# Attention scores of a hybrid decoder block: two 128-row matmuls per head become three pairs of 64-row matmuls, one head in each half of the array

## The chip, the cores and the metric

The kernel runs on one core of one Trainium2 chip (trn2). The metric is the device time of one execution in microseconds (us). Five engines work side by side: TensorE (PE) for matrix products, with its weight loads shown apart as PEld, VectorE (DVE), ScalarE (ACT), GpSimd (POOL) and SyncE (SP), which here only issues DMAs.

## The reference, cut to what matters

One decoder block on 2048 positions and 1024 channels. Two branches are computed from one input projection, gated, merged, projected and normalised. The part that is changed is the score product of the attention branch:

```python
q, k, v, g_attn, u_lru, g_lru, gate_logits = jnp.split(x @ w_in[l] + b_in[l], SPLIT_POINTS, axis=-1)
q, k = rope(q), rope(k)                     # 3 groups x 8 heads x 64 channels
for g, (window, dilation) in enumerate(((128, 1), (512, 4), (2048, 16))):
    # positions regrouped by residue mod dilation, blocks of 128 queries
    # against [previous block, current block] of keys
    s = jnp.einsum('brnqhd,brnkhd->brnhqk', qb, kw) * (Dh ** -0.5)
    s = jnp.where(valid, s, NEG_INF)
    m = jnp.max(s, -1); p = jnp.exp(s - m); l = jnp.sum(p, -1)
    o = jnp.einsum('brnhqk,brnkhd->brnqhd', p, vw) / l
# groups combined by their softmax weights, times silu(g_attn), projected;
# branch B: conv, gated linear recurrence; merge, output projection, layer norm
```

## The kernel before

The kernel has three stages. In the first (`product`, L583), PE multiplies x by the input projection, tile by tile of 128 x 512, each float32 operand split into a high and a low part of type fp32r, so that a product is three matmuls (high x high, high x low, low x high). The loop over `where` (L904 on) goes in ticks of 12 matmuls; a planner with budgets per engine (`left`, `Ask`, `chains`) places what follows each tile: rotary rotation, splits, stores to scratch in DRAM. q is stored there already split (`qh`, `ql`), k whole (`k`).

The second stage is the attention. A *unit* u is one pair of heads of one group, 12 units in the order of groups 0, 2, 1 (`unit`, L764). Each has 16 query blocks, so there are 192 steps, with m = 16u + n. In the loop at L1061 step m issues, in program order,

- `step_s(m)`: the scores of block n for both heads into PSUM, then on DVE the mask and row minimum (L977), on ACT the exponential (L979);
- `step_t(m-3)`: transposes of the 128 x 128 blocks of p on PE (L988) and their copy out of PSUM, by ACT (L993) or DVE (L995);
- `step_v(m-4)`: the products with v in float32, two instructions each (L1012), a copy every second step (L1016) and a store to `o_scr` every fourth (L1026).

A block with a previous block has 256 keys and twice the transposes and products with v. A block without one, and every block of group 2, has 128; in group 2 the score matmul still writes 256 columns.

For the scores, each head has its own full-height operands. `A[:, h]` holds `qh` of head h in its 64 partitions and `ql` in the other 64. `B1[:, h]` holds the high part of k in both halves, and `b2[:, h]` the low part of k in the head's half and zeros in the other. So two matmuls over 128 rows give qh·kh + ql·kh and qh·kl (L973). The zeros are written once (L780, L781). The k of a unit is loaded half by half into `b2`; POOL makes the high part (L792), copies it across (L793) and subtracts (L795), each on 64 x 1024 elements; for the first head of unit 0 ACT and DVE do that (L788, L789, L795).

Slots of SBUF are named by hand (`USLOT`, L757): three per unit, two units held. The parts of unit u+1 are queued in `loads` at n = 0 of unit u and one is issued per step (L1070 to L1075), since their slots are those of unit u-1. The first loads are issued in the last seven ticks of the first stage (L917), where slots become free as the x blocks in them are used for the last time, and just ahead of the loop (L1057): unit 1's q, then the v of group 2. All of these go through SP's queue in program order. `later(n, fn)` runs fn n ticks or steps on; the splits of k run 3 and 4 after their load. PSUM has three buffers for scores (both heads in one bank), three for transposes and two for o.

The third stage (`yb_job`, `combine`, `ya_job`, `out_job`) takes the slots X0 to X5 again; its first weights and inputs are loaded during unit 11 (L1076 to L1081).

Of the kernel before, what the change touches and what calls it, by code (L numbers as in the profile page):

```python
# [15 lines left out]
P = 128  # L16
# [15 lines left out]
def hybrid_block_kernel(ctx: ExitStack, tc: tile.TileContext, a: dict, out: bass.AP):  # L32
# [3 lines left out]
    def flat(t):  # L36
        return t.bitcast(F32)
# [45 lines left out]
    def big(slot, shape, dt, name):  # L83
        return (Y if slot[0] == "Y" else Z if slot[0] == "Z" else X).tile(shape, dt, name=name, tag=slot)
# [671 lines left out]
    lo_, up_ = slice(0, 64), slice(64, P)  # L756
    USLOT = (("X4", "X3", "X2"), ("Y0", "X1", "X0"))  # L757
    VSLOT = {(0, 0): "X5", (2, 0): "Y1", (1, 0): "Y2", (0, 1): "X5", (2, 1): "Y1", (1, 1): "Y2"}
    zero = [False, False]
    B2 = {}  # L760
# [7 lines left out]
    def unit_parts(u):  # L768

        sl = USLOT[u % 2]  # L770
        g, hp = unit(u)
        q = {n: qk_scr[n, 4 * g + hp] for n in ("qh", "ql", "k")}

        def k_part(h, hs, os):
            def fn():
                if h == 0:
                    units[u] = [None, big(sl[1], [P, 2, S], F32R, f"B{u}")]
                    if u < 2:
                        B2[u] = big(sl[2], [P, 2, S], F32R, f"C{u}")
                        pool.memset(flat(B2[u][up_, 0]), 0.0)  # L780
                        pool.memset(flat(B2[u][lo_, 1]), 0.0)  # L781
                    units[u].append(B2[u % 2])
                _, B1, b2 = units[u]
                sp.dma_start(flat(b2[hs, h]), q["k"][hs])

                def split(t):
                    if (u, h) == (0, 0):
                        act.activation(B1[hs, h, t], flat(b2[hs, h, t]), AF.Copy)  # L788
                        act.activation(B1[os, h, t], flat(B1[hs, h, t]), AF.Copy)  # L789
                        eng = dve  # L790
                    else:
                        pool.tensor_copy(B1[hs, h, t], flat(b2[hs, h, t]))  # L792
                        pool.tensor_copy(B1[os, h, t], flat(B1[hs, h, t]))  # L793
                        eng = pool
                    eng.tensor_tensor(out=b2[hs, h, t], in0=flat(b2[hs, h, t]), in1=flat(B1[hs, h, t]), op=ALU.subtract)  # L795

                later(3, lambda: split(slice(0, S // 2)))
                later(4, lambda: split(slice(S // 2, S)))
            return fn

        def q_part(hs, h, n, qs):
            def fn():
                if (hs, h) == (lo_, 0):
                    units[u][0] = big(sl[0], [P, 2, S], F32R, f"A{u}")
                sp.dma_start(flat(units[u][0][hs, h]), q[n][qs])
# [96 lines left out]
    first, second, firstv = unit_parts(0), unit_parts(1), v_parts(0, 0)  # L902
# [48 lines left out]
    def step_s(m):  # L951
        u, n = divmod(m, 16)
        g, _ = unit(u)
        A, B1, b2 = units[u]
# [6 lines left out]
        for h in range(2):  # L961
            q = A[:, h, n * P:(n + 1) * P]
            for i, B in enumerate((B1, b2)):
                if g == 2:
                    k = B[:, h].rearrange("p (c r i) -> p r c i", c=4, r=16)[:, max(n - 1, 0):n + 1]
                elif pv is None:
                    k = B[:, h, n * P:(n + 1) * P]
                elif g == 0:
                    k = B[:, h, (n - 1) * P:(n + 1) * P]
                else:  # L970
                    c, r = divmod(n, 4)
                    k = B[:, h, (c - 1) * CH:(c + 1) * CH].rearrange("p (c r j) -> p r c j", c=2, r=4)[:, r]
                pe.matmul(s[:, h, (0 if g == 2 and n else lo):256], q, k, start=(i == 0), stop=(i == 1))  # L973
        p = at_p.tile([P, 2, 256], F32, tag="p", name=f"p{m}", bufs=5)
        for h in range(2):
            mm = osb[:, n % 4, 130 + h:131 + h]
            dve.tensor_tensor_reduce(out=p[:, h, lo:256], in0=s[:, h, lo:256], in1=mask[:, lo:256],  # L977
# [79 lines left out]
    for fn in second[2:] + v_parts(2, 0):  # L1057
        fn()
    VORD = {0: (1, 0), 4: (0, 1), 5: (2, 1), 6: (1, 1)}
    loads = []  # L1060
    for m in range(NB + 4):  # L1061
# [8 lines left out]
        if n == 0 and 1 <= u <= 10:  # L1070
            loads += unit_parts(u + 1)
# [360 lines left out]
```

## Time and profile before

| | us |
|---|---|
| median of 3 runs | 2267.64 (2267.12 to 2272.91) |
| span of the profiled execution | 2268.7 |
| PE busy | 2213.9 (98%) |
| DVE busy | 1752.4 (77%) |
| ACT busy | 1091.3 (48%) |
| POOL busy | 874.6 (39%) |
| first to last score matmul | 1480.4 to 1807.6 |

The profiled execution is one run under the profiler. Its span, from the first to the last instruction, is the time that is known of it; it stands 1.1 us above the median of the runs. A matmul's duration runs from its start to a modelled end and overlaps the next one's, so the distance between starts, and not the duration, tells what a matmul costs in a dense row.

### The profile page before, as it was taken

How to read it: one execution, taken by the hardware profiler on the slowest of the kernel's cores; microseconds unless marked ns; L12 is line 12 of the kernel's file. 1: busy time of each engine (PE TensorE's matmuls, PEld its weight loads, DVE VectorE, ACT ScalarE, POOL GpSimd, SP SyncE). 2: the span in 40 equal slices, each digit the busy share in tenths (PEclk: the TensorE clock that was granted, in tenths of full speed). 3: DMA queues.
4: the chain of work that ended last, by engine and by line, in shares of the span. 5: the costliest groups of instructions: out<-in, count | busy, mean ns of one | idle time of the engine just before them, and what ended most of it. 6: DMA issues, size and time to landing. Idle time of an engine off the chain costs nothing.

```text
span 2268.7 us, 34220 instructions
## 1 busy us (share of the span) xinstructions
PE 2213.9 (98%) x11032; PEld 1868.7 (82%) x11032; DVE 1752.4 (77%) x3234; ACT 1091.3 (48%) x1982; POOL 874.6 (39%) x640
## 2 busy tenths in 40 slices
PE   7999999999999999999999999989999999999998
PEld 6888878888787788888888888878999888788887
DVE  8788878999898877778778878655666668967777
ACT  5344545456455656556566566555666621121010
POOL 1545544555454022222222212257676426722220
PEclk9999999999999999999999999999999999999999
DMA  7998897988987777686888787897786679884441
GB/s 227 268 259 254 244 266 222 273 267 269 273 266 249 258 215 225 201 241 208 252 276 258 249 250 237 251 256 176 206 217 160 191 234 316 287 271 167 130 140 65
DMA packets 327954, 526.01 MB, mean 232 GB/s; under 512 B 97120, under 2 KB 138080, under 8 KB 322912
## 3 DMA queue, kind: packets, MB, share of 16 engines
q1 hardware_dynamic: 297008, 479.05, 68.1%
q0 software_dynamic: 10080, 18.35, 5.1%
q10 hardware_dynamic: 20688, 26.42, 3.7%
q8 instruction: 88, 1.44, 0.3%
q14 instruction: 90, 0.74, 0.1%
HBM read 318.38 MB, written 190.64 MB: 224 GB/s over the span
## 4 chain that ended last, share of the span: by engine, by line
PE 57%; DMA 6%; DVE 2%; ACT 1%; POOL 1%; issue 1%; SPq 1%; ACTq 0%; DVEq 0%; POOLq 0%
PE q L598 29%; PE o L1012 4%; PE s L973 3%; PE z L1304 2%; PE z L1305 2%; PE z L1303 2%; PE yb L1198 2%; PE yb L1200 2%; PE yb L1199 2%; PE pt L988 2%; DMA A<-qh_scr 2%; PE ya L1271 1%; PE ya L1272 1%; PE ya L1270 1%; DMA l<-wl_scr 1%
## 5 line engine op out<-in xcount | busy, mean ns | idle before, releaser
L598 PE MATMUL q<-xT,hS 128*128 128x512 f32 x1680 | 520.9, 391 | 7.2 <-ACT e L621 6.0
L598 PE MATMUL q<-xT,l 128*128 128x512 f32 x1120 | 437.1, 390 | 0.0
L598 PE MATMUL q<-xB,hA 128*128 128x512 f32 x1248 | 389.7, 394 | 10.1 <-ACT xB L202 5.7
L598 PEld LDWEIGHTS q<-xT,hS 128*128 128x128 f32 x1680 | 314.9, 188 | 73.0 <-ACT e L621 6.4
L598 PE MATMUL q<-xB,l 128*128 128x512 f32 x904 | 354.6, 392 | 1.4 <-DMA l<-wl_scr 1.3
L598 PEld LDWEIGHTS q<-xB,hA 128*128 128x128 f32 x1248 | 234.7, 189 | 61.0 <-ACT xB L202 5.7
L598 PEld LDWEIGHTS q<-xT,l 128*128 128x128 f32 x1120 | 210.7, 188 | 44.1
L979 ACT ACTIVATE p<-p,osb 128x256 f32<-128x256 f32 (+1 forms) x384 | 156.2, 454 | 118.4 <-DVE osb L977 117.7
L214 POOL TENSOR_TENSOR S<-S,wA 128x512 f32<-128x512 f32 x35 | 45.7, 1306 | 422.6 <-DVE S L214 251.7
L977 DVE CUSTOM_DVE_ANT_0 p<-s,mask 128x256 f32<-128x256 f32 (+1 forms) x384 | 125.2, 364 | 103.0 <-PE s L973 61.5
L598 PEld LDWEIGHTS q<-xB,l 128*128 128x128 f32 x904 | 171.0, 189 | 38.5 <-DMA l<-wl_scr 2.2
L214 POOL TENSOR_TENSOR sw<-sw,sin 128x512 f32<-128x512 f32 x96 | 161.8, 1691 | 70.3 <-DMA sw<-y 64.6
L259 ACT ACTIVATE hA<-wA 128x512 fp32r<-128x512 f32 x218 | 135.5, 624 | 89.6 <-DMA wA<-in_w_in_dram 52.7
L598 PE MATMUL q<-xB,hS 128*128 128x512 f32 x560 | 174.9, 394 | 3.0 <-DVE v L214 3.0
L598 PE MATMUL q<-xT,hA 128*128 128x512 f32 x560 | 173.1, 390 | 3.1 <-ACT hi L323 1.8
L1012 PE MATMUL o<-V,ptb 128*128 128x65 f32 x1200 | 166.4, 277 | 8.0 <-ACT ptb L993 5.3
L1012 PEld LDWEIGHTS o<-V,ptb 128*128 128x128 f32 x1200 | 153.3, 196 | 19.4 <-ACT ptb L993 16.2
L259 ACT ACTIVATE hS<-S 128x512 fp32r<-128x512 f32 x175 | 109.2, 624 | 97.1 <-DVE S L214 51.3
L214 POOL TENSOR_TENSOR l<-wA,hA 128x512 fp32r<-128x512 f32 x68 | 105.2, 1547 | 80.3 <-ACT hA L259 61.6
L973 PE MATMUL s<-B,A 128*128 128x256 f32 (+1 forms) x384 | 116.8, 326 | 10.0 <-DMA A<-qh_scr 6.4
L598 PEld LDWEIGHTS q<-xT,hA 128*128 128x128 f32 x560 | 104.6, 188 | 26.6 <-issue 3.7
L598 PEld LDWEIGHTS q<-xB,hS 128*128 128x128 f32 x560 | 104.7, 189 | 25.1 <-issue 4.1
(196 smaller groups left out, 4853.0 us busy)
## 6 DMA issues: line engine op xcount, KB each, us to landing
wA<-in_w_in_dram SPq DMA_DIRECT2D x253, 256.0 KB, 5.0
wl_scr<-l SPq DMA_DIRECT2D x105, 512.0 KB, 5.3
l<-wl_scr SPq DMA_DIRECT2D x105, 512.0 KB, 4.7
sw<-y SPq DMA_DIRECT2D x384, 64.0 KB, 3.3
wS<-in_w_in_dram SPq DMA_DIRECT2D x70, 256.0 KB, 4.7
wS<-in_w_in_dram POOLq DMA_DIRECT2D x70, 256.0 KB, 6.6
o_scr<-osb ACTq DMA_DIRECT2D x48, 264.0 KB, 5.9
oc<-o_scr SPq DMA_DIRECT2D x48, 264.0 KB, 5.0
```

The lines of the kernel that those rows point to most:

```text
L214: eng.tensor_tensor(out=out, in0=in0, in1=in1, op=op)
L259: act.activation(h, r, AF.Copy)
L598: pe.matmul(bank, w[:, ks], x[:, kk, xx], start=(first and i == 0), stop=(last and i == 11))
L973: pe.matmul(s[:, h, (0 if g == 2 and n else lo):256], q, k, start=(i == 0), stop=(i == 1))
L977: dve.tensor_tensor_reduce(out=p[:, h, lo:256], in0=s[:, h, lo:256], in1=mask[:, lo:256], scale=1.0, scalar=3e38, op0=ALU.add, op1=ALU.min ...
L979: act.activation(p[:, h, lo:256], p[:, h, lo:256], AF.Exp, scale=-1.0, bias=mm)
L988: pe.transpose(pt[:, 2 * h + x, :], p[:, h, x * P:(x + 1) * P], ident)
L1012: pe.matmul(o[:, n % 2, h * 65:h * 65 + 65], ptb[:, 2 * h + x, :], V[:, kb, vo + h * 65:vo + h * 65 + 65], start=(x == lo // P), stop=(x = ...
L1198: pe.matmul(yb, WL[f][:, 0, k], xx[:, 0], start=(k == 0), stop=False)
L1199: pe.matmul(yb, WL[f][:, 0, k], xx[:, 1], start=False, stop=False)
L1200: pe.matmul(yb, WL[f][:, 1, k], xx[:, 0], start=False, stop=(k == 7))
L1303: pe.matmul(z, mh[:, k], w[:, 0, hs], start=(k == 0), stop=False)
```

## The change

The operands of a unit become two tiles of 128 partitions, in the layout in which q and k lie in DRAM: head 0 in partitions 0 to 63, head 1 in 64 to 127. `A[:, 0]` is `qh` and `A[:, 1]` `ql`, `B[:, 0]` the high part of k and `B[:, 1]` the low part. Each head's scores are three matmuls over its 64 partitions, issued in turn for the two heads, and each head's scores get a PSUM bank of their own. There are no zeros and no second copy of the high part, and the k parts are split in pieces of 128 x 512. With two slots a unit, three units are held: the parts of unit u+2 are queued at n = 1 of unit u, and unit 2 is loaded ahead of the loop, behind the v of group 2. PSUM buffers for scores go from three (both heads each) to four (one head each), those for transposes from three to two.

```diff
-    USLOT = (("X4", "X3", "X2"), ("Y0", "X1", "X0"))
+    HALF = (slice(0, 64), slice(64, P))
+    USLOT = (("X3", "X2"), ("X0", "X4"), ("Y0", "X1"))
...
-        def k_part(h, hs, os):
+        def k_part(j):
+            cols = slice(j * S // 2, (j + 1) * S // 2)
+
+            def split(t):
+                K = units[u][1]
+                if u == 0:
+                    act.activation(K[:, 0, t], flat(K[:, 1, t]), AF.Copy)
+                    eng = dve
+                else:
+                    pool.tensor_copy(K[:, 0, t], flat(K[:, 1, t]))
+                    eng = pool
+                eng.tensor_tensor(out=K[:, 1, t], in0=flat(K[:, 1, t]), in1=flat(K[:, 0, t]), op=ALU.subtract)
+
             def fn():
...
+                if j == 0:
+                    units[u][1] = big(ks, [P, 2, S], F32R, f"B{u}")
+                sp.dma_start(flat(units[u][1][:, 1, cols]), q["k"][:, cols])
+                for i in range(2):
+                    c0 = (2 * j + i) * CH
+                    later(3 + i, lambda c0=c0: split(slice(c0, c0 + CH)))
             return fn

-        def q_part(hs, h, n, qs):
+        def q_part(i, n):
...
-                sp.dma_start(flat(units[u][0][hs, h]), q[n][qs])
+                sp.dma_start(flat(units[u][0][:, i]), q[n])
...
-        return [k_part(0, lo_, up_), k_part(1, up_, lo_), q_part(lo_, 0, "qh", lo_), q_part(up_, 0, "ql", lo_),
-                q_part(lo_, 1, "ql", up_), q_part(up_, 1, "qh", up_)]
+        return [k_part(0), k_part(1), q_part(0, "qh"), q_part(1, "ql")]
...
-            for fn in ((), (), first[:2], first[2:], firstv, second[:1], second[1:2])[j]:
+            for fn in ((), first[:2], first[2:], second[:2], firstv, second[2:], ())[j]:
...
-        s = aps.tile([P, 2, 256], F32, tag="s", name=f"s{m}", bufs=3)
+        s = [aps.tile([P, CH], F32, tag="s", name=f"s{m}{h}", bufs=4) for h in range(2)]
...
-        for h in range(2):
-            q = A[:, h, n * P:(n + 1) * P]
-            for i, B in enumerate((B1, b2)):
+        for i, (x, y) in enumerate(((0, 0), (1, 0), (0, 1))):
+            for h, hs in enumerate(HALF):
+                q, K = A[hs, x, n * P:(n + 1) * P], B[hs, y]
...
-                pe.matmul(s[:, h, (0 if g == 2 and n else lo):256], q, k, start=(i == 0), stop=(i == 1))
+                pe.matmul(s[h][:, (0 if g == 2 and n else lo):256], q, k, start=(i == 0), stop=(i == 2))
...
-        pt = aps.tile([P, 4, P], F32, tag="t", name=f"pt{m}", bufs=3)
+        pt = aps.tile([P, 4, P], F32, tag="t", name=f"pt{m}", bufs=2)
...
-    for fn in second[2:] + v_parts(2, 0):
+    for fn in v_parts(2, 0) + third:
...
-        if n == 0 and 1 <= u <= 10:
-            loads += unit_parts(u + 1)
+        if n == 1 and 1 <= u <= 9:
+            loads += unit_parts(u + 2)
```

More of the change, by code (lines that the diff above doesn't have):

```diff
@@ L768, in unit_parts @@
     def unit_parts(u):
-        sl = USLOT[u % 2]
+        qs, ks = USLOT[u % 3]
         g, hp = unit(u)
         q = {n: qk_scr[n, 4 * g + hp] for n in ("qh", "ql", "k")}
-        def k_part(h, hs, os):
-            def fn():
[L776 to L798, printed above, removed]
@@ L900, in hybrid_block_kernel @@
     at(10, lambda: start_chain(scales()))
-    first, second, firstv = unit_parts(0), unit_parts(1), v_parts(0, 0)
+    first, second, third, firstv = unit_parts(0), unit_parts(1), unit_parts(2), v_parts(0, 0)
     low = NS
@@ L953, in step_s @@
         g, _ = unit(u)
-        A, B1, b2 = units[u]
+        A, B = units[u]
         pv = prev(g, n)
         lo = 0 if pv is not None else P
-        s = aps.tile([P, 2, 256], F32, tag="s", name=f"s{m}", bufs=3)
+        s = [aps.tile([P, CH], F32, tag="s", name=f"s{m}{h}", bufs=4) for h in range(2)]
         if n % 4 == 0:
```

18 lines of the change are left out of this document (8 added, 10 removed).

## The prediction

> **What bounds the kernel now.** I read the page first, then the attention stage alone, because the change touches nothing else.
>
> ```profile
> PE 2213.9 (98%) x11032; PEld 1868.7 (82%) x11032; DVE 1752.4 (77%) x3234; ACT 1091.3 (48%) x1982; POOL 874.6 (39%) x640
> ...
> PE q L598 29%; PE o L1012 4%; PE s L973 3%; PE z L1304 2%; PE z L1305 2%; PE z L1303 2%; PE yb L1198 2%; PE yb L1200 2%; PE yb L1199 2%; PE pt L988 2%; DMA A<-qh_scr 2%; PE ya L1271 1%; PE ya L1272 1%; PE ya L1270 1%; DMA l<-wl_scr 1%
> ```
>
> PE is the bound. The chain that ended last holds the score matmuls (s, L973) and, unusually, the load of q (A<-qh_scr, 2% of the span). The busy times by stretch show where that load matters:
>
> ```profile
> 1508.20:1515.00 6.80, 1.15 (x7) 0.86 (x7) 0.79 (x2) 0.45 (x2) 6.23 (x4) 0.82 0.72 276
> 1515.00:1520.00 5.00, 5.00 (x28) 5.00 (x28) 1.02 (x8) 2.16 (x6) 0.00 (x0) 0.56 0.86 271
> ...
> 1538.90:1543.00 4.10, 0.58 (x6) 0.47 (x5) 0.64 (x4) 0.96 (x3) 3.96 (x4) 1.00 1.08 274
> 1543.00:1549.00 6.00, 6.00 (x32) 6.00 (x32) 2.30 (x14) 2.62 (x8) 5.72 (x5) 0.53 1.00 220
> 1549.00:1785.00 236.00, 231.70 (x1945) 222.99 (x1944) 148.65 (x705) 155.31 (x386) 156.42 (x106) 0.99 0.74 190
> ```
>
> The columns are the stretch, its length, the busy times of PE, PEld, DVE, ACT and POOL, the granted clock, the DMA share and GB/s. From 1549 to 1785 PE is busy in 231.7 of 236 us, DVE in 148.7 and ACT in 155.3: PE sets the pace. Twice PE is empty, at the starts of units 1 and 2, and each time the clock then stands near half, at 0.56 over 5 us and 0.53 over 6 us. The timeline of PE names what it waited for:
>
> ```profile
> 1512.21 0.33 PE L973 MATMUL s<-B,A 128*128 128x128 f32 x1 [3.57 <-POOL B L793]
> 1514.62 0.48 PE L973 MATMUL s<-C,A 128*128 128x128 f32 x1 [2.08 <-POOL C L795]
> ...
> 1542.82 0.30 PE L973 MATMUL s<-B,A 128*128 128x128 f32 x1 [3.52 <-DMA A<-qh_scr]
> ```
>
> Unit 1 waits 5.65 us for POOL's split of k, unit 2 waits 3.52 us for q. At a clock of 0.56 and 0.53 the slow stretches lose 5 x 0.44 = 2.2 and 6 x 0.47 = 2.8 us. That is 14.2 us in all which a change of loads alone could bring back.
>
> **The price of a matmul.** A step with 256 keys, on PE:
>
> ```profile
> 1640.25 0.36 PE L973 MATMUL s<-B,A 128*128 128x256 f32 x1
> 1640.45 0.28 PE L973 MATMUL s<-C,A 128*128 128x256 f32 x1
> 1640.57 0.29 PE L973 MATMUL s<-B,A 128*128 128x256 f32 x1
> 1640.69 0.28 PE L973 MATMUL s<-C,A 128*128 128x256 f32 x1
> 1640.81 0.60 PE L988 MATMUL pt<-ident,p 128*128 128x128 f32 x4
> 1641.25 1.00 PE L1012 MATMUL o<-V,ptb 128*128 128x65 f32 x8
> 1642.06 0.36 PE L973 MATMUL s<-B,A 128*128 128x256 f32 x1
> ```
>
> The starts give 0.20 + 3 x 0.12 = 0.56 us for four scores, 0.44 for four transposes and 0.81 for eight products with v, 1.81 in all. Columns hardly matter here: the score matmuls of 128 columns at the start of unit 0 stand just as far apart, while 512 columns take twice that:
>
> ```profile
> 1483.60 0.30 PE L973 MATMUL s<-B,A 128*128 128x128 f32 x1 [2.88 <-DMA A<-qh_scr]
> 1483.73 0.29 PE L973 MATMUL s<-C,A 128*128 128x128 f32 x1
> ```
>
> ```profile
> 850.14 2.74 PE q L598 x12
> ```
>
> 2.74 / 12 = 0.23 us for 512 columns, but 0.13 for 128 and 0.12 for 256. So up to 256 columns the price is a slot of about 0.12 us for one weight load with its matmul; the slot, not the streaming, is paid. The first score of a step costs 0.08 more, at the passage from the float32 products with v to fp32r scores.
>
> **The change, part by part.** *Scores.* Four matmuls become six, in three pairs. No row of this trace has fewer than 128 rows, so a pair is bounded by its neighbours: one slot of 0.12 us if its two halves load and run together, two slots, 0.24, if the weight loads go one after the other. Less than one slot I exclude but for the 0.10 of the products with v (0.81 / 8). Three pairs then take from 0.36 to 0.72 us against 0.48, that is -0.12 to +0.24 per step. I take -0.12: the halves share no partition of the operands and no PSUM bank, and the rows show loads running beside matmuls all through the stage (PEld busy 222.99 beside PE 231.70). [...]
>
> *Which steps gain.* The counts of the masked minimum and what follows it, by shape:
>
> ```profile
> L977 DVE CUSTOM_DVE_ANT_0 p<-s,mask 128x256 f32<-128x256 f32 x216 | 83.0, 422 | 51.6 <-PE s L973 28.4 <-ACT ptb L993 18.0 <-ACT p L979 2.5
> L979 ACT ACTIVATE p<-p,osb 128x128 f32<-128x128 f32 x168 | 58.4, 395 | 56.1 <-DVE osb L977 55.5
> L977 DVE CUSTOM_DVE_ANT_0 p<-s,mask 128x128 f32<-128x128 f32 x168 | 42.2, 289 | 51.4 <-PE s L973 33.1 <-ACT p L979 11.8 <-PE pt L988 5.3
> ...
> L1016 DVE COPY osb<-o 128x260 f32<-128x260 f32 x96 | 41.0, 427 | 28.6 <-PE o L1012 28.2
> ...
> L977 DVE DVE_READ_ACCUMULATOR2_ANT osb<- 128x1 f32 x384 | 31.9, 83 | 0.0
> ...
> L993 ACT ACTIVATE ptb<-pt 128x256 f32<-128x256 f32 x54 | 19.5, 361 | 0.0
> ...
> L995 DVE COPY ptb<-pt 128x256 f32<-128x256 f32 x30 | 12.6, 420 | 0.0
> ```
>
> 216 / 2 = 108 wide steps and 168 / 2 = 84 narrow ones. A wide step is PE's alone. In the narrow ones of group 2 another engine is near:
>
> ```profile
> 1530.06 0.37 PE L973 MATMUL s<-B,A 128*128 128x256 f32 x1
> ...
> 1531.21 0.36 PE L973 MATMUL s<-B,A 128*128 128x256 f32 x1
> ...
> 1532.28 0.66 PE L1012 MATMUL o<-V,ptb 128*128 128x65 f32 x4
> 1532.75 0.37 PE L973 MATMUL s<-B,A 128*128 128x256 f32 x1
> ...
> 1533.90 0.36 PE L973 MATMUL s<-B,A 128*128 128x256 f32 x1
> ```
>
> Steps of 1.15, 1.54 and 1.15 us: in one of three the products with v come late, behind the copy of p's transposes. Three such steps take 3.84 us, in which DVE works 6 x (0.289 + 0.083) + 0.420 + 1.5 x 0.427 = 3.29 us and ACT 6 x 0.395 + 2 x 0.361 = 3.09. PE's gain of 0.36 would leave 3.48, hardly more than DVE needs, so I take half, 0.06 per narrow step (bounds 0 and 0.12).
>
> *Loads and splits.* The bytes stay: 1 MB of k and 2 MB of q a unit, in four DMAs for six. POOL's work shrinks:
>
> ```profile
> L795 POOL TENSOR_TENSOR C<-C,B 64x1024 fp32r<-64x1024 f32 x45 | 106.4, 2365 | 3.2
> ...
> L793 POOL CAST B<-B 64x1024 fp32r<-64x1024 f32 x45 | 46.7, 1037 | 2.8
> L792 POOL CAST B<-C 64x1024 fp32r<-64x1024 f32 x45 | 46.5, 1034 | 92.6 <-DMA C<-k_scr 78.2 <-ACT p L979 13.6
> ```
>
> 4 x (2.365 + 1.037 + 1.034) = 17.7 us a unit become four copies and four subtractions on half as many columns, an estimate of 4 x (0.52 + 1.18) = 6.8 us. POOL is off the path except at unit 1. There unit 1's k is issued before unit 0's v, so it lands some 20 us before it is wanted. SP's queue and the DMAs of the start:
>
> ```profile
> 1514.67 3.74 SPq L824 DMA_DIRECT2D V<-v_scr  x4
> ...
> 1535.18 1.18 SPq L805 DMA_DIRECT2D A<-qh_scr  x1
> ```
>
> ```profile
> DMA packets 7918, 19.34 MB, mean 245 GB/s; under 512 B 664, under 2 KB 4760, under 8 KB 6706
> ...
> V<-v_scr SPq DMA_DIRECT2D x12, 520.0 KB, 11.0
> ...
> A<-qh_scr SPq DMA_DIRECT2D x8, 512.0 KB, 12.3
> ```
>
> The second answer covers 1464 to 1543: 19.34 MB at 245 GB/s, so the start is bound by transfers. The last of three v tiles (L824, 4 x 520 KB = 2.13 MB) is issued before unit 2's q and is needed later than it. The change puts unit 2 ahead of that tile: 2.13 MB / 245 GB/s = 8.7 us earlier, so q lands at 1534.1 instead of 1542.8.
>
> Does PE get there by then? Unit 0 still begins at 1483.6, since what it needs is first in the queue before and after. The 1 MB of unit 1's k now stands ahead of its v, which comes 4.3 us later; I put 2 us of waiting on that (0 to 4). Unit 0's 16 steps took until 1508.2; less 16 x 0.12 = 1.9, plus 2, is 1508.3. Unit 1 ran from 1514.6 to 1538.9, 24.3 us with 2.2 of slow clock, so 22.1, less 16 x 0.06 = 1.0: PE is at unit 2 at 1529.4 and waits till 1534.1. Gain up to here: 8.7 us, and what the scores save in units 0 and 1 is inside it. The slow clock after that wait I leave in.
>
> *Queues and buffers.* In the loop unit u+2 is asked for at n = 1 of u, when u-1 has let go of its slots; four issues pass SP's queue in place of six, always ahead of the v parts of n = 7, and land a unit early. SP runs further ahead of PE at the end, where the slots X2 and X3 for the third stage's first weights come free one unit sooner; no wait of PE hangs on them that I count. Two steps' scores instead of three now fit in PSUM: a score matmul waits for the row minimum two steps back, and behind it in PE's queue stand a transpose and a product with v. DVE does these minima within 0.75 us, two narrow steps are 2.3: cost zero, up to 0.1 per narrow step (8 us) if DVE lags. Two transpose buffers cost nothing by order: the products with v of m-4 already wait for the copy that frees the buffer for the transposes after them. Splits of unit 0 on ACT and DVE stay about as long in columns (4 x 512 each).
>
> **Sum.** Of the 160 steps after unit 2's start 93 are wide and 67 narrow: 93 x 0.12 + 67 x 0.06 = 11.2 + 4.0 = 15.2 us. With 8.7 that is 23.9, from 2268.7 to 2244.8; the profiled run lies 1.1 above the median, so I say 2244 us. This case alone reaches from 2228 (the 0.08 at the passage gone too, no stall left at units 1 and 2) to 2257 (narrow steps gain nothing, wide ones 0.04).
>
> **The rivals.** *Entering and leaving the halves costs time* (2277). If the array must be empty before it changes between full height and halves, a matmul starts after the end of the last one, 0.28 us after its start, and not after 0.12: 0.16 at each of two passages a step, of which 0.08 is paid already at one. That is +0.24 - 0.12 = +0.12 a step, 160 x 0.12 = 19.2; units 0 and 1, slower by 1.9 each, reach unit 2 at about 1536, which leaves 6.8 of the stall's gain and ends its slow clock (2.8): 2268.7 + 19.2 - 9.6 - 1.1 = 2277. It decides once a passage costs over 0.09 us more than now. For it speaks that one passage, float32 to fp32r, already costs 0.08; against, that scores to transposes costs nothing (0.12). [...]
>
> *Weight loads of the two halves take turns* (2300). Six slots: +0.24 a step, 160 x 0.24 = 38.4; PE then comes to unit 2 at 1540, which leaves 2.8 of the gain and ends the slow clock: 2268.7 + 38.4 - 5.6 - 1.1 = 2300. For it speaks that a slot in this stage is as long for 65 columns as for 256, so the loads, and not the columns, fill it. Nothing in the trace speaks against it, since no load of half height is in it. With the empty array on top, +0.48 a step: about 2346.
>
> *The pairs do not pay and do not hurt* (2259): the slots stay at 0.56 and only the loads give their 8.7.
>
> **How the numbers follow.** Forecast 0.42; rival of passages 0.22; loads in turn 0.22, and with passages 0.08; loads alone 0.06. The range, 2228 to 2306, holds all but the double rival and the tails of the others. About 0.3% (7 us) is what a measurement of this kernel can tell from no change. Faster: nearly all of 0.42 and 0.06 and the low end of the passages (0.03), 0.49. Same: 0.08, from the passages' middle. Slower: 0.43.
>
> **What would show it.** Right: the score pairs start 0.12 us apart with the two of a pair together, wide steps of 1.69, no wait on POOL at unit 1, unit 2's wait ending near 1534, POOL busy some 125 us less (199.6 in the three rows against 11 x 6.8). Wrong: starts of all six 0.12 apart (loads in turn); a gap above 0.2 before the first score or the first transpose (passages); a new wait of s on DVE L977 (two buffers); a wait for V in unit 0 over 4 us.

## The result, and the profile after

The changed kernel takes 2279.62 us (median of four runs, 2277.79 to 2281.31) against 2267.38 us before (2266.56 to 2272.91, four runs): a ratio of 1.0054, 95% interval 1.0039 to 1.007. It is 12 us slower, where 24 us faster was forecast. The run whose profile follows took 2278.78 us. The time lies 3 us from the passages rival's 2277, but the experiments show that it gets there by another sum. Several kernels with half-height matmuls, further down, differ from run to run by up to 10% with the granted clock (`one_half`: 2343.27 us at 0.985, 2582.39 us at 0.883); for these the spread is given.

The page after, the same rows as before:

```profile
PE 2240.3 (98%) x11416; PEld 1863.7 (82%) x11416; DVE 1756.1 (77%) x3236; ACT 1089.3 (48%) x1982; POOL 746.0 (33%) x586
...
PE q L598 49%; PE o L1005 6%; PE s L966 4%; PE pt L981 4%; PE z L1298 3%; PE z L1296 3%; PE z L1297 3%; PE yb L1191 2%; PE yb L1193 2%; PE yb L1192 2%; PE ya L1265 1%; PE ya L1264 1%; PE ya L1263 1%; DVE y L214 1%; PE vtp L349 1%
```

The load of q has left the chain that ended last, and POOL is busy 128.6 us less. PE is busy 26.4 us more: nothing new is waited for, PE's own work has become longer, and 30.7 us of it run at a granted clock of 0.50, as the stretches will show. PE's waits from 1476 to 1850 us, as the totals, the number of times and the longest, say the same:

```profile
PE o L1005 <- ACT ptb L986: 2.6, 4, 1.9
PE o L1005 <- DVE ptb L988: 1.1, 1, 1.1
PE s L966 <- DVE y L214: 0.3, 1, 0.3
```

The waits of units 1 and 2 for POOL and for q are gone. Now the stretches, cut where units begin (L966's first matmul of a unit). After: unit 0, unit 1, unit 2, units 3 to 10, and unit 11 in two pieces.

```profile
1478.10:1505.30 27.20, 26.39 (x241) 22.91 (x240) 17.20 (x75) 18.19 (x41) 13.31 (x15) 1.00 1.04 405
1505.30:1529.00 23.70, 23.70 (x215) 20.32 (x214) 13.53 (x78) 13.85 (x42) 7.36 (x8) 1.00 0.65 226
1529.00:1556.00 27.00, 26.86 (x243) 23.38 (x242) 16.92 (x78) 18.00 (x45) 7.37 (x8) 1.00 0.43 160
1556.00:1775.00 219.00, 218.54 (x1974) 191.09 (x1972) 130.89 (x619) 136.51 (x341) 51.61 (x56) 1.00 0.51 180
1775.00:1788.90 13.90, 10.87 (x95) 8.70 (x94) 9.62 (x41) 8.95 (x24) 0.00 (x0) 0.99 0.79 266
1788.90:1819.40 30.50, 30.49 (x153) 27.75 (x154) 12.29 (x46) 14.34 (x31) 10.17 (x8) 0.50 0.12 42
```

The same units before: 0, 1, 2, 3 to 10, and unit 11.

```profile
1480.40:1508.20 27.80, 24.28 (x207) 23.50 (x206) 17.25 (x76) 18.16 (x41) 16.32 (x13) 1.00 1.05 250
1508.20:1538.90 30.70, 24.56 (x185) 23.32 (x184) 13.55 (x77) 13.97 (x42) 16.58 (x12) 0.89 0.86 247
1538.90:1572.10 33.20, 29.26 (x212) 28.55 (x212) 17.13 (x80) 18.01 (x45) 24.88 (x17) 0.85 0.59 151
1572.10:1778.40 206.30, 202.79 (x1719) 195.32 (x1718) 129.86 (x618) 136.59 (x340) 141.23 (x96) 1.00 0.77 196
1778.40:1807.60 29.20, 26.51 (x199) 25.15 (x199) 20.52 (x83) 21.53 (x51) 10.12 (x8) 0.88 0.53 182
```

Three things are to be seen. Unit 3 begins at 1556.0 instead of 1572.1, 16.1 us earlier. Units 3 to 10 then take 219.0 us instead of 206.3, at a granted clock of 1.00 in both: 12.7 us given back. Unit 11 takes 40.6 us up to its last score (1815.6) instead of 29.2: from 1788.7 on PE works at half clock (0.50) for 30.7 us, with no idle time in it (30.49 of 30.50 us busy). Before, the same place had 6.8 us of half clock. So 16.1 - 12.7 - 11.4 is about -8 at the last score; the slow clock reaches 4 us further, to 1819.4.

A wide step of the changed kernel, to be held against the one that the prediction shows:

```profile
1640.23 0.62 PE L966 MATMUL s<-B,A 64*128 64x256 f32 x6
1640.78 0.66 PE L981 MATMUL pt<-ident,p 128*128 128x128 f32 x4
1641.27 1.00 PE L1005 MATMUL o<-V,ptb 128*128 128x65 f32 x8
1642.20 0.62 PE L966 MATMUL s<-B,A 64*128 64x256 f32 x6
```

It takes 1.98 us (1640.226 to 1642.204) instead of 1.81. From the single starts in the trace: the three pairs begin at 1640.226, 1640.449 and 1640.567, the two of a pair 3 to 4 ns apart. Before, the starts of the four scores were 0.20, 0.12 and 0.12 apart, and the first transpose came 0.12 after the last: 0.56. The three pairs are 0.22 and 0.12 apart, and the first transpose comes 0.21 after the last: 0.55. Ahead of them, from the last product with v to the first score, are 0.205, where 0.084 were; behind them, from the first transpose to the first product, 0.493, where 0.436 were. So the pairs save one slot (-0.12), and the passages cost 0.02 + 0.09 inside the scores, 0.12 ahead of them and 0.06 behind: 0.29, which leaves the step 0.17 longer. A sign of it shows in the weight loads: before, those of the first transpose (1640.71, matmul 1640.81) ran ahead, beside the last score. Now the load begins with its matmul (1640.775 and 1640.777), and so does the first score's (1640.225 and 1640.226; before, 1640.221 and 1640.250).

### The profile page after: what moved, and what is told of

Same layout as the page of the kernel before. It is cut to its first block, busy times and chain, and to the rows that moved or that the text cites. A ratio compares the mean times of both kernels' runs of the same rounds, so it can differ in the third digit from the quotient of the medians.

```text
span 2277.0 us, 34843 instructions
## 1 busy us (share of the span) xinstructions
PE 2240.3 (98%) x11416; PEld 1863.7 (82%) x11416; DVE 1756.1 (77%) x3236; ACT 1089.3 (48%) x1982; POOL 746.0 (33%) x586
## 4 chain that ended last, share of the span: by engine, by line
PE 84%; DVE 6%; DMA 5%; issue 2%; ACT 1%; SPq 1%; POOL 0%; DVEq 0%; ACTq 0%; POOLq 0%
PE q L598 49%; PE o L1005 6%; PE s L966 4%; PE pt L981 4%; PE z L1298 3%; PE z L1296 3%; PE z L1297 3%; PE yb L1191 2%; PE yb L1193 2%; PE yb L1192 2%; PE ya L1265 1%; PE ya L1264 1%; PE ya L1263 1%; DVE y L214 1%; PE vtp L349 1%
## 5 line engine op out<-in xcount | busy, mean ns | idle before, releaser
L970 DVE CUSTOM_DVE_ANT_0 p<-s,mask 128x256 f32<-128x256 f32 (+1 forms) x384 | 125.2, 364 | 106.4 <-PE s L966 77.7
L214 POOL TENSOR_TENSOR l<-wA,hA 128x512 fp32r<-128x512 f32 x68 | 105.8, 1556 | 86.5 <-ACT hA L259 70.3
L966 PE MATMUL s<-B,A 64*128 64x256 f32 (+1 forms) x1152 | 121.1, 316 | 0.4 <-DVE y L214 0.3
```

What stands on the lines that cost most here:

```text
L214: eng.tensor_tensor(out=out, in0=in0, in1=in1, op=op)
L966: pe.matmul(s[h][:, (0 if g == 2 and n else lo):256], q, k, start=(i == 0), stop=(i == 2))
L970: dve.tensor_tensor_reduce(out=p[:, h, lo:256], in0=s[h][:, lo:256], in1=mask[:, lo:256], scale=1.0, scalar=3e38, op0=ALU.add, op1=ALU.min ...
```

## The experiments

Steps are compared at full clock throughout. Comments in the diffs below do not stand in the kernels, and `...` marks a gap in a diff.

The theory after the result: passages between full and half height cost more than the pairs save, the rest of the change is worth much more than 8.7 us, and the clock in unit 11 takes some of that. The rivals: the halves' weight loads take turns; the slow clock is the loads' doing; the rest gains only what was forecast.

**The loads alone, and the scores alone.** `loads_alone` keeps everything of the change but the pairs:

```diff
-        for i, (x, y) in enumerate(((0, 0), (1, 0), (0, 1))):
-            for h, hs in enumerate(HALF):
-                q, K = A[hs, x, n * P:(n + 1) * P], B[hs, y]
+        for h in range(2):
+            for i in range(2):
+                q, K = A[:, h, n * P:(n + 1) * P], B[:, i]
...
-                pe.matmul(s[h][...], q, k, start=(i == 0), stop=(i == 2))
+                pe.matmul(s[h][...], q, k, start=(i == 0), stop=(i == 1))
```

> The changed kernel with its tiles, loads, splits and buffers, but with four score matmuls over all 128 partitions in place of the six over 64 (it leaves out the separation of the two heads, so the scores are not the reference's). Theory (the loss is the passages between half and full height, the loads gain): wide steps 1.81 us again instead of 1.98, no wait at units 1 and 2, unit 3 begins about 16 us earlier than before; 2248 to 2256 us. Rival (the smaller buffers for scores and transposes hold PE up): wide steps stay near 1.97 and the time near 2280.

Measured: 2241.2 us (2238.87 to 2246.12), ratio 0.9882 (0.9863 to 0.9902). So the layout, the loads and the PSUM buffers are worth 27 us, three times the 8.7 of the forecast, and the pairs with what hangs on them cost 38. Its stretches, units 3 to 10 and unit 11:

```profile
1550.30:1749.60 199.30, 198.45 (x1718) 194.74 (x1718) 129.20 (x619) 136.36 (x341) 51.81 (x56) 1.00 0.55 198
1749.60:1778.50 28.90, 26.46 (x200) 25.32 (x200) 20.07 (x83) 21.58 (x51) 10.22 (x8) 0.88 0.43 148
```

Against these, the change loses 219.0 - 199.3 = 19.7 us in units 3 to 10, 5.7 in units 0 to 2 (unit 3 begins at 1550.3 here) and 11.7 in unit 11. Two later kernels give the price of the pairs without unit 11's slow clock: the change with unit 11 mended (`wl_apart`) takes 2265.5 us and single matmuls with the same mend (`full_wl`) 2238.1, so the pairs cost 27 us by themselves.

`scores_alone` puts the pairs, and a bank for each head, on the layout of before:

```diff
-        for h in range(2):
-            q = A[:, h, n * P:(n + 1) * P]
-            for i, B in enumerate((B1, b2)):
+        for i, (x, B) in enumerate(((0, B1), (1, B1), (0, b2))):
+            for h, hs in enumerate((lo_, up_)):
+                q, K = A[hs, h ^ x, n * P:(n + 1) * P], B[hs, h]
```

> The kernel before with its tiles and loads, but with scores as three pairs over 64 partitions, a bank per head and the buffers of the change (the low part of q is taken from the other head, so the scores are not the reference's). Theory: wide steps 1.97 us, +0.16 each; the waits at units 1 and 2 remain or shrink a little since PE comes later; the clock falls in unit 11 and stays low as in the changed kernel: 2285 to 2300 us. Rival (the six matmuls cost no more than four, the loss is in the loads or in unit 11 alone): 2265 to 2272.

Measured: 2343.46 us (2327.08 to 2503.26), ratio 1.0312 (1.0245 to 1.0378). A wide step is 1.98 us here as well, so the passages do not hang on the layout. The rest is clock:

```profile
1485.70:1591.50 105.80, 105.80 (x544) 93.06 (x543) 39.84 (x189) 39.88 (x103) 51.58 (x36) 0.50 0.66 168
1591.50:1837.30 245.80, 243.39 (x2199) 212.82 (x2199) 147.14 (x689) 154.05 (x382) 142.44 (x97) 1.00 0.69 182
1837.30:1850.00 12.70, 11.98 (x60) 10.55 (x59) 7.24 (x27) 7.62 (x16) 5.08 (x4) 0.50 0.28 105
```

After the wait of 2.62 us for q at the start of unit 0, PE stays at half clock for 105.8 us, in which it is never idle. In the kernel before, the stalls of units 1, 2 and 11 were followed by 6.8, 10.2 and 6.8 us of half clock.

**Do the halves overlap?** `one_half` puts both heads' matmuls on partitions 0 to 63, so that no two of them lie in different halves (with the mended unit 11 of `wl_apart`, below):

```diff
-                q, K = A[hs, x, n * P:(n + 1) * P], B[hs, y]
+                q, K = A[HALF[0], x, n * P:(n + 1) * P], B[HALF[0], y]
```

> As wl_apart, but both heads' score matmuls read partitions 0 to 63 (head 1's scores are those of head 0, not the reference's), so no two of them can lie in different halves of the array. Theory (halves run together, and PE finds the pairs itself, which is why the order by head cost nothing): six slots of 0.11 instead of three, wide steps about 2.3 us, 2325 to 2335 us. Rival (a matmul of half height takes half a slot, with no overlap): unchanged, 2265.

```profile
1600.41 0.97 PE L966 MATMUL s<-B,A 64*128 64x256 f32 x6
1601.32 0.66 PE L981 MATMUL pt<-ident,p 128*128 128x128 f32 x4
1601.81 1.00 PE L1005 MATMUL o<-V,ptb 128*128 128x65 f32 x8
1602.74 0.97 PE L966 MATMUL s<-B,A 64*128 64x256 f32 x6
```

Measured: 2343.27 to 2582.39 us. The six scores take 0.97 instead of 0.62, three slots of 0.117 more, and a wide step 2.33. So in the change the halves do overlap; the rival of loads in turn is out.

`by_head` issues head 0's three matmuls and then head 1's:

```diff
-        for i, (x, y) in enumerate(((0, 0), (1, 0), (0, 1))):
-            for h, hs in enumerate(HALF):
+        for h, hs in enumerate(HALF):
+            for i, (x, y) in enumerate(((0, 0), (1, 0), (0, 1))):
```

> The changed kernel with the three score matmuls of head 0 ahead of those of head 1, so that neighbours sit in the same half of the array. Theory (the two halves run together when they alternate): three slots of 0.12 us more a step, wide steps about 2.3 us, about 2340 us. Rival (the halves do not run together even now, and the six matmuls cost what they cost): unchanged, 2280.

```profile
1641.44 0.56 PE L966 MATMUL s<-B,A 64*128 64x128 f32 x6
1641.93 0.66 PE L981 MATMUL pt<-ident,p 128*128 128x128 f32 x4
```

Measured: 2283.35 us (2280.87 to 2284.47), ratio 1.0064 (1.0047 to 1.008), steps of 1.98. A miss: the order costs nothing. The six, here with 128 columns, take 0.56 us, against 0.55 for six such matmuls of the change, and the single starts are 1641.438 and 1641.448, 1641.602 and 1641.612, 1641.714 and 1641.725. So the starts come in pairs 0.010 to 0.011 us apart in this order too, while six of one half stand 0.117 apart (`one_half`). The trace does not name the half of a matmul: that a pair holds one matmul of each half, the second ahead of two that were issued before it, is the author's reading and was not shown.

**The passages.** `third_late` adds a second round trip to a step, by issuing the third pair behind the transposes:

```diff
...
+                if i < 2:
+                    mm()
+                else:
+                    st["last"].append(mm)
+        if m >= 3:
+            step_t(m - 3)
+        for mm in st.pop("last"):
+            mm()
```

> As wl_apart, but the third pair of a step's scores is issued behind the transposes, so a step has four passages instead of two. Theory: 0.26 us more a step, 192 x 0.26 = 50 us, about 2315 us, provided the clock stays full. Rival (passages cost little): about 2265.

```profile
1600.83 0.50 PE L968 MATMUL s<-B,A 64*128 64x256 f32 x4
1601.26 0.66 PE L991 MATMUL pt<-ident,p 128*128 128x128 f32 x4
1601.85 0.39 PE L968 MATMUL s<-B,A 64*128 64x256 f32 x2
1602.17 1.11 PE L1015 MATMUL o<-V,ptb 128*128 128x65 f32 x8
1603.20 0.50 PE L968 MATMUL s<-B,A 64*128 64x256 f32 x4
```

Measured: 2351.75 to 2577.63 us. A wide step takes 2.37 us, 0.39 more for a second round trip with the same matmuls. The first one costs 0.29 more than the single matmuls paid, and these paid 0.08 at a passage already: 0.37. The price is the passage's: in these runs 0.37 to 0.39 us for there and back. What PE does in that time they do not show.

**Unit 11.** `wl_apart` puts the low part of the next stage's first weights on DVE one step later than ACT's high part, so that neither holds up the copies of p's transposes:

```diff
-            later(lag, lambda ks=ks: split(t[:, 0, ks], t[:, 1, ks], 0.5))
+            later(lag, hi)        # act.activation(t[:, 0, ks], ..., AF.Copy, scale=0.5)
+            later(lag + 1, lo)    # dve.scalar_tensor_tensor(out=t[:, 1, ks], ...)
```

> The changed kernel, with the low part of the third stage's first weights computed on DVE one step after ACT's high part, so that DVE does not wait for ACT in unit 11. Theory (one idle stretch of PE halves the clock, which then stays down till the next stage, 9 steps of 3.58 us instead of 1.98): no wait of 1.9 us in unit 11, full clock to the end of the stage, 14 us less, about 2265 us. Rival (the clock falls because pairs of half height keep PE less busy, not because of the wait): the clock falls all the same, about 2279.

> The kernel before with the later low part of the first weights, as in wl_apart. Theory (full-height scores bring the clock back within 7 us, so the wait in unit 11 costs little there): the 4.7 us that unit 11's three steps lose, about 2263 us. Rival: 14 us as in the changed kernel, 2254.

Measured: `wl_apart` 2265.52 us (ratio 0.9981, 0.997 to 0.9993), `before_wl`, the same edit on the kernel before, 2263.13 us (ratio 0.9972, 0.9957 to 0.9986). In the changed kernel it is worth 14 us by the medians and 17 by the ratios, in the one before 6 to 7. In both the idle time it removes is small. In the changed kernel PE waited 1.93 and 1.08 us for copies, up to 1786.0 and 1788.9, and the clock fell at 1788.7; the kernel before waited 2.31 us. With the edit 0.58 and 0.41 us remain, the clock stays at 1.00, and unit 11 takes 26.8 us:

```profile
1774.90:1801.70 26.80, 25.78 (x229) 22.00 (x230) 20.17 (x81) 21.39 (x51) 10.22 (x8) 1.00 0.46 160
```

So a stall of about the same size costs the half-height kernel some 7 to 10 us more.

**Where the 27 us come from.** `loads_64` is `loads_alone` with each load in two, of 64 partitions each, and `full_onebank` is `loads_alone` with before's PSUM buffers (both heads in one bank):

```diff
+                for hs in HALF:
+                    sp.dma_start(flat(units[u][0][hs, i]), q[n][hs])      # loads_64, k the same way
...
+        s = aps.tile([P, 2, 256], F32, tag="s", name=f"s{m}", bufs=3)     # full_onebank; pt bufs=3
```

> As loads_alone (2241.2 us; four matmuls of full height, which leaves out the separation of the heads), but each load of q and k is two DMAs over 64 partitions, as before. Theory (a DMA over 64 partitions moves its bytes at some 230 GB/s, one over 128 at some 410): the rate at the start falls to 230 to 260 GB/s, unit 0 starts 2 to 3 us later, and a wait comes back at unit 1 or 2: 2246 to 2262 us. Rival (the rate comes from the order and number of the loads): 400 GB/s and 2241.

> As loads_alone (2241.2 us; four matmuls of full height, which leaves out the separation of the heads), but with the score and transpose buffers of the kernel before: both heads in one bank, three buffers each. Of the 27 us that loads_alone is under the kernel before, some 7 lie in units 3 to 10, where nothing waits for loads: narrow steps that were 1.54 us are 1.30, wide ones of 1.89 are 1.81. Theory (a bank per head lets DVE start earlier): these steps come back, 2246 to 2250 us. Rival (POOL's smaller share of the work does it): they stay away, 2241.

Measured: `loads_64` 2248.79 us, ratio 0.9909 (0.9886 to 0.9932); `full_onebank` 2250.9 us, ratio 0.9925 (0.9901 to 0.9949). From `loads_64`, PE's waits:

```profile
PE o L1007 <- ACT ptb L988: 6.7, 6, 3.5
PE s L968 <- DMA A<-ql_scr: 5.1, 1, 5.1
PE o L1007 <- DMA V<-v_scr: 1.8, 1, 1.8
```

and the transfers from 1464 to 1543 us, of `loads_alone` and then of `loads_64`:

```profile
DMA packets 9692, 25.93 MB, mean 328 GB/s; under 512 B 736, under 2 KB 4832, under 8 KB 8403
```

```profile
DMA packets 8490, 19.25 MB, mean 244 GB/s; under 512 B 772, under 2 KB 4868, under 8 KB 7714
```

The rate goes with the width of the transfers: 244 GB/s with loads over 64 partitions, 328 over 128. `loads_64` has twice as many loads too, but the trace's packets tell the two apart: in this stretch a packet of 8192 bytes on SP's queue took 557 ns on average in `loads_64` and 567 before, but 315 in `loads_alone` and 317 in the change. In unit 0 the kernel before moved 250 GB/s and the changed one 405, both with all engines' time taken (DMA share 1.05 and 1.04 in the stretches above); the prediction kept before's 245 for the new loads. Why a packet takes longer in the narrower transfer was not shown.

The bank, with the buffer numbers that go with it, is worth about 9.7 us. In the narrow steps here every other one has the products with v late in `full_onebank`:

```profile
1510.20 0.73 PE L966 MATMUL s<-B,A 128*128 128x256 f32 x4
...
1511.27 0.66 PE L1005 MATMUL o<-V,ptb 128*128 128x65 f32 x4
1511.74 0.48 PE L966 MATMUL s<-B,A 128*128 128x256 f32 x2
```

A step of 1.54, as before the change, with the products 0.51 behind the transposes at 1510.76; in `loads_alone` the steps there are 1.14 to 1.30. `before_banks` checks the bank by itself on the kernel before, and `before_order` adds an order of loads (with the split of `before_wl` in both):

```diff
+        s = [aps.tile([P, CH], F32, tag="s", name=f"s{m}{h}", bufs=4) for h in range(2)]   # both; pt bufs=2
...
-            for fn in ((), (), first[:2], first[2:], firstv, second[:1], second[1:2])[j]:
+            for fn in ((), (), first[:2], first[2:], second[:2] + firstv, (), ())[j]:      # before_order
```

> The kernel before with wl's split apart and with the one part of the change that the 27 us of its gain side is thought to owe most to: a PSUM bank for each head's scores (four s, two t) in place of one bank for both; scores stay single matmuls of 128 rows, loads and their order stay. Theory (the bank is worth about 9.7 us whatever the loads are): about 2263 - 10 = 2253 (2248 to 2258), the narrow steps of the units at 1.15 to 1.30 us instead of 1.15 to 1.54. Rival (the bank helps only where the loads of the change have made room): 2260 to 2266.

> before_banks with the order of the loads mended by hand: k of unit 1 queued ahead of v of unit 0, and v of group 1 behind unit 2's parts. Layout of 64 partitions, single matmuls of 128 rows, all arithmetic in place. Theory: the waits of units 1 and 2 that the kernel before shows go, and unit 0 waits about 2 us more for v: about 2253 - 12 = 2241 (2235 to 2250), below both kernels. Rival (the queue at 245 GB/s is the limit of units 0 to 2, so an order only moves the wait): 2250 to 2256.

Measured: `before_banks` 2251.89 us, ratio 0.9926 (0.9909 to 0.9944); against `before_wl`'s 0.9972 that is 10 us, as expected. In the wide step at 1640 us of the kernel before, VectorE's first row minimum starts 0.87 us after the first score, 0.15 behind the end of the fourth matmul; in `before_banks`, in the step at 1641.4, it starts 0.63 us after, 0.15 behind the end of that head's own two. In the kernel before the two heads also share one tile; whether the bank or the tile made VectorE wait was not parted. `before_order` 2247.77 us, ratio 0.9901 (0.9883 to 0.9919): 4 more by the medians and 6 by the ratios, where 12 were expected. POOL's wait of unit 1 and the wait of unit 2 for q are gone, but behind a late copy in unit 1's last steps the clock stands at 0.50 for 10.2 us:

```profile
1532.36 0.66 PE L1012 MATMUL o<-V,ptb 128*128 128x65 f32 x4 [1.83 <-ACT ptb L993]
```

```profile
1533.90:1544.10 10.20, 10.20 (x52) 10.20 (x51) 5.01 (x27) 4.96 (x16) 1.60 (x2) 0.50 1.02 280
```

So 10 of the 27 us are the bank, 6 to 8 the width of the transfers. The other 9 to 11 I put down to the order of the loads and to less work on POOL. They were not parted further, but they lie at the start: units 3 to 10 take 198.8 us in `before_banks`, with before's loads and POOL's full work, and 199.3 in `loads_alone`, against 206.3 before and 206.6 in `full_onebank`. There the bank is the whole gain.

**Fewer passages.** If the passage is the price, scores of two or four steps together should pay it once for two or four. Three forms were tried: scores of two steps in turn with their row minima (`two_steps`), row minima after both (`two_steps_b`, `four_steps_b`), and the products with v two steps behind their transposes instead of one (`two_steps_c`, `four_steps_c`). All have the split of `wl_apart`.

```diff
+        if m % 2 == 0:        # two steps of a head share a bank
+            st["s"] = [aps.tile([P, CH], F32, tag="s", name=f"s{m}{h}", bufs=4) for h in range(2)]
+        s = [b[:, m % 2 * 256:m % 2 * 256 + 256] for b in st["s"]]
...
+        if m % 2 == 0:        # four_steps: 4; p bufs=8
+            for soft in [step_s(k) for k in range(m, m + 2) if k < NB]:
+                soft()        # row minima and exponentials
+            for k in range(m - 3, m - 1):
+                if 0 <= k < NB:
+                    step_t(k)
+                if 0 <= k - 2 < NB:      # _b: k - 1
+                    step_v(k - 2)
```

> The changed kernel with the later low part of the first weights (as in wl_apart, 2265.5 us) and with the scores of two steps issued together, then transposes and products with v of two steps: half as many passages between half and full height; two steps of a head share a bank. Theory (a pair of passages costs 0.26 us a step): 0.13 less per step, 192 x 0.13 = 25 us, about 2240 us, under both kernels. Rival (the passages cost little, the longer wide steps come from the six matmuls or the smaller buffers): 2260 to 2270, or slower.

> As two_steps, but the score matmuls of both steps come ahead of the row minima of both. In two_steps the second step's matmuls waited 0.6 us for DVE to read the bank that the two steps share, and the clock fell again and again. Theory (passages halved, no wait for the bank): wide steps 1.84 us, full clock, 192 x 0.13 = 25 us under wl_apart, about 2240 us. Rival (the gain of fewer passages goes into waits of PE for DVE and ACT, since their work comes in lumps): idle stretches of PE, the clock falls and stays down, over 2300 us.

> As two_steps_b with four steps together, a quarter of the passages. Theory: 192 x 0.20 = 37 us under wl_apart, about 2228 us, if DVE's and ACT's lumps stay covered by the transposes and products with v of four steps. Rival: PE waits at the lumps, the clock falls, over 2300 us.

> The score pairs of two steps together, so that one passage to half height and back serves two steps, with the products with V two steps behind their transposes instead of one, so that TensorE need not wait for the copies of pt (44.9 us in the run with one behind). Theory (passages cost, and only the copies stood in the way): a wide step of about 1.85 us at full clock and about 2265 - 22 = 2243 (2235 to 2255). Rival (the clock falls in a stretch of half-height matmuls once anything has let TensorE idle, and does not come back): 2300 to 2400 with granted clocks under 0.98 and no wait on ACT named.

> The score pairs of four steps together, products with V two steps behind their transposes. Theory (a step pays the 0.26 us of passages once in four): a wide step of about 1.98 - 0.19 = 1.79 to 1.75 us against 1.81 of two steps together, 160 steps x 0.05 = 8 us less than the 2238.8 of that run, so about 2231 (2225 to 2245). Rival (twelve half-height pairs in a row let the clock fall, or the row minima of four steps come too late for the transposes): 2290 to 2350, with waits on ACT or DVE named or granted clocks under 0.98.

> The change with four score matmuls of 128 rows a step (q's and k's rows not multiplied as the reference wants: the layout does not hold a head in 128 rows, so its outputs are not the reference's) and wl's split apart: the yardstick for the pairs of two and four steps. Theory: 2241.2 of the run without the split apart less 4 = 2237 (2232 to 2243), so that pairs of two steps together gain nothing against single matmuls. Rival (the split apart gives nothing where the clock comes back at once): 2241 to 2246.

Measured: `two_steps` 2530.21 us (1.1056, 1.0999 to 1.1113), `two_steps_b` 2384.76 (1.0513, 1.0454 to 1.0572), `four_steps_b` 2338.51 (1.0321, 1.027 to 1.0372), `two_steps_c` 2238.78 (0.9864, 0.9844 to 0.9884), `four_steps_c` 2273.79 (1.0017, 1.0004 to 1.0031), `full_wl`, single matmuls of 128 rows and a yardstick only, 2238.09 (0.9868, 0.9847 to 0.9888). PE's longest wait from 1476 to 1850, for `two_steps`, `two_steps_b`, `two_steps_c` and `four_steps_c` in this order:

```profile
PE s L968 <- DVE osb L972: 38.8, 69, 0.7
```

```profile
PE o L1010 <- ACT ptb L991: 42.8, 47, 1.8
```

```profile
PE pt L986 <- ACT ptb L991: 3.5, 3, 2.4
```

```profile
PE pt L986 <- ACT ptb L991: 28.4, 30, 2.1
```

In the first, the second step's scores waited in the shared bank for DVE to read the first's. In the second, the products came too soon behind their transposes. Slow clock came on top, 416 us of it in `two_steps` from 1484 us on, 160 in `two_steps_b` between 1542 and 1918. With both waits gone, the clock stays full (1.00 from 1481.3 to 1774.0) and the passages are paid once for two steps:

```profile
1640.59 0.98 PE L968 MATMUL s<-B,A 64*128 64x256 f32 x12
1641.50 0.66 PE L986 MATMUL pt<-ident,p 128*128 128x128 f32 x4
1641.99 1.00 PE L1010 MATMUL o<-V,ptb 128*128 128x65 f32 x8
1642.83 0.60 PE L986 MATMUL pt<-ident,p 128*128 128x128 f32 x4
1643.27 1.00 PE L1010 MATMUL o<-V,ptb 128*128 128x65 f32 x8
1644.21 0.97 PE L968 MATMUL s<-B,A 64*128 64x256 f32 x12
```

3.62 us for two steps, 1.81 each: 0.17 below the change's step, which is about half of the 0.37 for a round trip. `two_steps_c` is 41 us faster than the change, by the medians, 14 of them by the mended unit 11, and 1.4% faster than the kernel before. Against `full_wl` it gains nothing: at one round trip for two steps the pairs have just earned back their passages. With four together, the passages do go down further: the three groups of four wide steps without a wait and at full clock take 6.88 us each, 1.72 a step. But ACT comes too late with its copies (37 us of waits with DVE's 8.9) and the clock falls seven times between 1486 and 1807, for 41 us in all. That a version without these waits would beat 2238 was not shown.

## Why the prediction was wrong

- **The step that failed: "I take -0.12".** The term priced the passages at nothing. The pairs did what it says (two together, one slot saved of four), but passages cost 0.29: +0.17 a wide step instead of -0.12. The argument against the rival was that scores to transposes cost nothing; that row (0.12) has both at full height, and with the scores at half height the same gap is 0.21. The rival's own price, +0.24 for two passages, came within 0.05, in part by luck: it had 0.08 more at the scores and 0.16 at the transposes, and the trace has 0.12 and 0.09, with 0.08 more inside the pairs and behind the first transpose. That the array has to be empty there was the rival's assumption, and no run shows it; the runs show the price alone, 0.29 us more a step and 0.37 to 0.39 for there and back.
- **Which steps gain.** The narrow steps were given half a slot, since DVE and ACT stand near. They became longer, 1.31 to 1.39: units 7 and 10, all narrow steps, take 23.7 us each instead of 22.3, and 21.3 in `loads_alone`. The late products with v there (1.54) had a cause that the change removes beside the pairs, the PSUM buffers with both heads in one bank (1.54 again in `full_onebank`, 1.14 to 1.30 in `loads_alone`). I had listed the new banks as a risk at best; they were worth about 10 us.
- **Loads: right in kind, mis-sized.** "8.7 us" should have been 27 with the bank, or about 17 without it. Unit 2 began at 1529.0, without waiting, where 1534.1 was forecast: the term moved the queue at before's 245 GB/s, while transfers over 128 partitions ran at 405. That PE was forecast to come there at 1529.4 is luck: unit 0 began at 1478.1 and not at 1483.6, since its wait for q went too, and units 0 and 1 took 27.2 and 23.7 us for the 24.7 and 21.1 of the forecast. With the stalls went their slow clock, which the sum had left in. My own bound, 14.2 us for the stalls and their clock, was the better number, and it was read too small: the half clock after unit 2's wait lasted 10.2 us and not 6, which loses 5.1 instead of 2.8 and makes the bound about 16.5. Unit 3 began 16.1 us earlier even with longer steps.
- **POOL:** forecast 125 us less, measured 128.6. No wait of s on DVE L970 came, and no wait for V in unit 0: both as priced, at nothing.
- **Unit 11 had no term.** "No wait of PE hangs on them that I count" was said of the third stage's first weights. A stall was there before (2.3 us) and after (3.0). What was not foreseen is its price: the half clock lasted 30.7 us instead of 6.8. Unit 11 took 11.7 us more than in `loads_alone`, some 2 of them for the passages in it. The prediction priced slow clock only where it would disappear.
- **The sum as it went:** -27 for layout, loads and banks, +25 for passages (19.7 + 5.7), +12 for unit 11, mostly its clock: +10 of the +12 measured. The rival's 2277 was met with its gain and its loss both too small, so its closeness is luck. (By its own terms the forecast's upper bound of its own case is 2255 and not 2257: 2268.7 - 8.7 - 93 x 0.04 - 1.1. Nothing hangs on it.)

## What to carry to other kernels

In this kernel matmuls on halves of the array gained something only where many of them stood together (a wide step at full clock took 1.98 us with a round trip in each, 1.81 with one for two steps, 1.72 with one for four; 1.81 with single matmuls in `loads_alone`): count the round trips to full height, not the matmuls, and price each round trip from a run of its own. A change that packs matmuls can also alter what a stall costs, as it did here (unit 11's was worth 14 us after and 6 to 7 before), so remove the small waits of PE first and look at the granted clock behind each. A change of layout moves things that no matmul shows, such as the number of partitions of a transfer (6 to 8 us here) or the PSUM buffers of the scores (about 10 us here); price these as terms of their own.

## What was unexpected in the hardware

- With a half-height passage in every step, the clock came back late or not in the stage, though PE was idle for at most 0.5 us in it: 30.7 us (the change), 37.5 (`by_head`), 105.8 (`scores_alone`). With full-height matmuls, after stalls of 1.8 to 5.7 us, it took 6.8 to 10.2 us (before, `before_order`, `loads_alone`), and with the passages of four steps in one (`four_steps_c`) seven falls took 41 us in all. `third_late` lost it at 1744.4, with PE busy all the time:

```profile
1740.00:1744.40 4.40, 4.40 (x35) 3.44 (x36) 2.30 (x14) 2.69 (x8) 2.23 (x3) 1.00 0.90 307
1744.40:1970.00 225.60, 225.60 (x972) 172.61 (x972) 71.09 (x305) 76.52 (x174) 22.64 (x22) 0.50 0.21 73
```

  `one_half` lost the clock too, at 1833.0 for 51.2 us, with PE busy all the time. It has as many passages as `wl_apart`, whose ten runs kept a granted clock of 0.995 or more, and single matmuls in place of the pairs; so the number of passages alone does not decide it. What does was not shown.
- Issued head by head (`by_head`), the matmuls still started in pairs, 0.010 to 0.011 us apart, and the step stayed at 1.98 us. That PE starts matmuls of the other half ahead of program order is the reading above, not shown.
- A matmul of 64 rows took the same slot as one of 128 (0.117 us in `one_half`, 0.12 in the kernel before): what the pairs gain here is their overlap (0.62 us for six in the change, 0.97 in `one_half`).
